# Rotation table: one more pause behind each quarter's stores; GLU products of the first tile one block later

## The chip, the core and the metric

The kernel runs on one core of a Trainium2 chip. The metric is device time in microseconds (us) from start to end of one execution. TensorE (PE) multiplies matrices and has a weight-load side (PEld), VectorE (DVE) and ScalarE (ACT) work on vectors, GpSimd (POOL) does little here, and SyncE (SP) issues nearly all DMAs, in order.

## The reference

A trunk of two layers, float32, 512 tokens of width 1024. Each layer is a SwiGLU feed-forward net (FFN, inner width 2752), a token mixer, and a second FFN; each of the three adds to the residual `x` behind an RMSNorm with shift, scale and gate from a conditioning vector. The second layer's mixer is a bidirectional complex-diagonal state-space model with a GLU:

```python
def s5_mixer(h, ...):
    u = h.reshape(Bsz, S, SSM_GROUPS, SSM_GROUP_DIM)          # 64 groups of 16
    y = d_skip * h
    for direction in range(N_DIRS):
        ar, ai, bb_re, bb_im = zoh_discretise(...)
        bu_re = jnp.einsum('bsgh,gph->bsgp', u, bb_re)        # and bu_im
        xr, xi = complex_linear_scan(ar, ai, bu_re, bu_im, reverse=(direction == 1))
        y = y + einsum(xr, c_re) - einsum(xi, c_im)
    y = jax.nn.gelu(y)
    z = y @ w_glu + b_glu                                     # 1024 x 2048
    return z[..., :D] * jax.nn.sigmoid(z[..., D:])
```

## The kernel before

Activations are held transposed, as 8 tiles of 128 channels by 512 tokens. A float32 product is made of three matmuls on operands that are split into a high and a low part (`mm3`, lines 684 to 686): high weight by low activation, high by high, low weight by high activation. For each weight tile the DMA brings `raw`, ACT casts the high part `whi` (line 677), and DVE makes the low part `wlo` by a subtraction (line 678). `raw` has 3 buffers, and `whi` and `wlo` have 4 each, so weights are prepared up to four tiles ahead of PE.

Every engine runs its instructions in the order in which the Python code emits them. Work for later stages is put between by generators: `prep()` advances the generator at the head of a list by one step (to its next `yield`), `mods()` makes one column of a modulation vector (line 635, with a DMA of `mw` behind it).

**The rotation table.** During the first FFN of layer 2, `rotation` builds the phases by which the mixer's states are turned. It works in four quarters. A quarter starts a tile `R` (one buffer, used by all four), doubles it six times with complex products (`cmul`, lines 127 to 129), and stores it into the DRAM scratch `rd` with four DMAs (line 279). Steps end at the `yield` inside the loops: the first step of a quarter holds the start and the doublings up to width 8 (24 small products behind two initial writes, L264 and L265 or L267 and L268); the three others hold six products of 256 columns each. Behind the last of these the generator is resumed once more: the stores go out, and the next quarter starts in the same step. The initial writes must wait until the stores have read `R`. Text below calls these steps *start step* and *product steps*.

In this FFN the hidden tiles are worked through in three parts (8, 7 and 6 tiles and a remainder of 64). In a part, first come the input products, 48 matmuls for each hidden tile, and then the output products, one for each of the 8 tiles of `x` (called d = 0 to 7), which in the second part have 21 matmuls each. In the output loop, each d has on DVE: the column of `mw`, the update of `x` (line 758), a step of the generator, and `wlo` of a later weight tile. The generator's later steps load the operators of the mixer's first blocks into SBUF (`rt`, `w1`, `w2`); `operators`, called behind d = 0 of the third part, runs what is left of it.

**The mixer.** `s5_mixer` goes over 8 blocks of 8 groups. `s5_state` of a block is 64 matmuls (line 1139), then on DVE the turning by `rt`, two scans (line 1161) and the turning back into `X`. `s5_out` (lines 1199 and 1207) makes the block's output from `u` and `X`; `s5_turn` (line 1222) transposes it, and ACT makes its GELU and the high part `hhi`; the low part `hlo` (line 1229) is put off to the end of the iteration (`self.lows`). Iteration b emits: output of block b, turning of block b-1, state of block b+2, the low part of block b-1, and then the share of block b-2 in the GLU's first tile: `glu_mm` with three matmuls for each of the two halves q. In iteration 7 the first five blocks' share of the GLU's second tile comes ahead of the output (30 matmuls). `glu` makes the rest.

Of the kernel before, what the change touches and what calls it, by code (L numbers as in the profile page):

```python
# [21 lines left out]
KD = D // P  # L22
# [42 lines left out]
class S5Prep:  # L65
# [155 lines left out]
    def rotation(self, pool):  # L221


        nc, I = self.nc, self.I
        v = nc.vector
        n = NG
        lam = pool.tile([P, 3, n], F32, name="lamB")
        nc.sync.dma_start(out=lam, in_=I["lamB"])
        yield
        S = lambda nm: pool.tile([P, n], F32, name=nm)  # L230
        dt, x1, th, si = (S(q) for q in ("dt", "x1", "th", "si"))
        self.vexp(pool, dt, lam[:, 2], n)
        yield
        v.tensor_tensor(out=x1, in0=lam[:, 0], in1=dt, op=ALU.mult)
        self.vexp(pool, self.rho, x1, n)
        for _ in range(3):
            v.tensor_tensor(out=self.rho, in0=self.rho, in1=self.rho, op=ALU.mult)
        v.tensor_tensor(out=th, in0=lam[:, 1], in1=dt, op=ALU.mult)
        v.tensor_scalar(out=th, in0=th, scalar1=8.0, scalar2=None, op0=ALU.mult)

        back = slice(n // 2, n)
        W = pool.tile([P, 2, 6, n], F32, name="W")
        self.vsincos(pool, W[:, 0, 0], si, th, n)
        yield
        v.tensor_copy(out=W[:, 1, 0, 0:n // 2], in_=si[:, 0:n // 2])
        v.tensor_scalar(out=W[:, 1, 0, back], in0=si[:, back], scalar1=-1.0, scalar2=None, op0=ALU.mult)
        yield
        for j in range(5):
            self.cmul(pool, W[:, 0, j + 1], W[:, 1, j + 1], W[:, 0, j], W[:, 1, j], W[:, 0, j], W[:, 1, j], [P, n])
        yield  # L250
        cur = W[:, 0, 0], W[:, 1, 0]
        for j in range(1, 6):
            o = [S(q) for q in (("dt", "x1"), ("th", "si"))[j % 2]]
            self.cmul(pool, *o, *cur, W[:, 0, j], W[:, 1, j], [P, n])
            cur = o
            if j % 2:
                yield
        nq = 4 * HB
        for q in range(NG // nq):
            gs = slice(q * nq, (q + 1) * nq)  # L260
            d, b0 = divmod(4 * q, NB)
            R = pool.tile([P, 2, nq, NC], F32, name="R")
            if d == 0:
                v.memset(R[:, 0, :, 0:1], 1.0)  # L264
                v.memset(R[:, 1, :, 0:1], 0.0)  # L265
            else:
                v.tensor_copy(out=R[:, 0, :, 0], in_=cur[0][:, gs])  # L267
                v.tensor_scalar(out=R[:, 1, :, 0], in0=cur[1][:, gs], scalar1=-1.0, scalar2=None, op0=ALU.mult)  # L268
            for j in range(6):
                w = 1 << j  # L270
                c = min(w, 16)
                bc = [W[:, r, j, gs].unsqueeze(2).to_broadcast([P, nq, c]) for r in range(2)]
                for i in range(0, w, c):
                    self.cmul(pool, R[:, 0, :, w + i:w + i + c], R[:, 1, :, w + i:w + i + c],
                              R[:, 0, :, i:i + c], R[:, 1, :, i:i + c], bc[0], bc[1], [P, nq, c])
                    if j > 2:
                        yield
            for b in range(4):
                nc.sync.dma_start(out=self.rd[b0 + b, :, d], in_=R[:, :, b * HB:(b + 1) * HB])

    def blocks(self, pool, psum, ident, eye16, dskip):

# [166 lines left out]
class Trunk:  # L449
# [865 lines left out]
    def s5_mixer(self, l, pool, pre, right, ops0, ut, rest):  # L1315
        nc, W = self.nc, self.W

        w1, w2, rt, w3, X = *ops0, {}
        pools = (pre, right)
        d0 = [pool.tile([P, 2, HB, NC + 1], F32, name=f"d{d}") for d in range(2)]  # L1320
        z = pool.tile([P, 2, HB, NC + 1], F32, name="z")
        wt = pool.tile([P, 2 * HB * (NC + 1) + 1], F32, name="ws")
        self.scan = d0, z, wt
        for t in (*d0, z):
            nc.gpsimd.memset(t[:, :, :, NC:NC + 1], 0.0)
        nc.gpsimd.memset(wt[:, 0:1], 0.0)
        for b in range(2, 4):
            w1[b] = self.s5_w1(pool, b, 2)
        r = self.s5_rstd(HALVES[1])
        for o in rest:  # L1330
            o()
        r()
        for b in range(len(ut), NB):
            ut[b] = self.s5_in(b)
        u = [self.s5_norm(ut[b], b) for b in range(2)]
        self.s5p = pools[0]
        self.gps = [[self.newps() for q in range(2)]]
        self.yv = []
        yj = {}
        for b in range(2):  # L1340
            X[b] = self.s5_state(pool, w1.pop(b), rt[b], u[b], b)
            w1[b + 4] = self.s5_w1(pools[b], b + 4)
            if b:
                while len(W.ready) < 4:
                    W.prep()
                yj[0] = self.s5_out(pool, w2.pop(0), w3.pop(0), ut[0], X.pop(0), 0)
            u.append(self.s5_norm(ut[b + 2], b + 2))
        self.lows = []
        self.gw = [[W.get(), W.get()] for m in range(2)]

        def turn(b):
            self.yv.append(tuple(t.rearrange("p (j c) -> p j c", j=L) for t in self.s5_turn(yj.pop(b))))

        for b in range(NB + 1):
            if 2 <= b <= 4:
                W.issue()
            if b == NB - 2:
                self.s5_spare(0)
            if b == NB - 1:
                self.s5_spare(1)  # L1360
                self.gps.append([self.newps() for q in range(2)])
                for q in range(2):
                    self.glu_mm(self.gps[1][q], self.gw[1][q], range(NB - 3))
            if 0 < b < NB:
                yj[b] = self.s5_out(pool, w2.pop(b), w3.pop(b), ut[b], X.pop(b), b)
            if b > 0:
                turn(b - 1)
            if b + 2 < NB:
                rt[b + 2] = self.s5_rt(pools[b % 2], b + 2)
                w3[b + 2] = self.s5_w3(pools[b % 2], b + 2)  # L1370
                w2[b + 2] = self.s5_w2(pools[b % 2], b + 2)
                if b + 4 < NB:
                    u.append(self.s5_norm(ut[b + 4], b + 4))
                X[b + 2] = self.s5_state(pool, w1.pop(b + 2), rt[b + 2], u[b + 2], b + 2)
                if b + 6 < NB:
                    w1[b + 6] = self.s5_w1(pool, b + 6, 2)
            while self.lows:
                self.lows.pop(0)()
            if b > 1:
                for q in range(2):  # L1380
                    self.glu_mm(self.gps[0][q], self.gw[0][q], [b - 2])

    def glu_mm(self, ps, w, ks, c0=0, c1=NC):
        n = L * (c1 - c0)
# [4 lines left out]
    def glu(self, l):  # L1389
# [4 lines left out]
        mm = self.glu_mm  # L1394

        def gate_in(m, ps):
            sg = self.tp.tile([P, T], F32, name="tmp")
            nc.scalar.activation(out=sg, in_=ps, func=AF.Sigmoid,
                                 bias=self.cols[:, C_GLUB + KD + m:C_GLUB + KD + m + 1], scale=1.0)
            return sg  # L1400
# [11 lines left out]
        def mods():  # L1412
            for _ in range(2):
                self.ahead = min(self.ahead, sum(not callable(t) for t in self.modq) - KD)
                if self.ahead or callable(self.modq[0]):
                    self.mods()

        for m in range(KD - 2):
            w = self.gw[m] if m < 2 else [W.get(), W.get()]
            ps = self.gps[m] if m < 2 else [self.newps() for q in range(2)]  # L1420
            if m == 0:
                for q in range(2):
                    mm(self.gps[1][q], self.gw[1][q], range(NB - 3, KD - 1))
                for q in range(2):
                    mm(ps[q], w[q], [KD - 1])
                sg = gate_in(m, ps[0])
                W.adv()
            else:
                ks = range(KD - 1 if m == 1 else 0, KD)
                mm(ps[0], w[0], ks)  # L1430
                sg = gate_in(m, ps[0])
                if m != 2:
                    W.adv()
                mods()
                mm(ps[1], w[1], ks)
            mix(m, ps[1], sg)
            if m != 2:
                W.adv()
            mods()

        a, b, hc = KD - 2, KD - 1, NC // 2
        w, sg = {}, {}
        for m in (a, b):
            w[m] = [W.get(), W.get()]
            ps = self.newps()
# [6 lines left out]
        for m in (a, b):  # L1452
            ps = self.newps()
            mm(ps, w[m][1], range(KD), 0, hc)
            mix(m, ps, sg[m], 0, hc)
        ps = {m: self.newps() for m in (a, b)}
# [310 lines left out]
```

## Time and profile before

| | us |
|---|---|
| median of three runs | 1734.79 |
| lowest and highest run | 1731.52 and 1735.48 |
| profiled execution | 1731.77 |
| its span, first to last instruction | 1729.8 |
| PE busy in the span | 1669.4 (97%) |
| DVE, ACT, POOL busy | 1186.2, 555.8, 100.1 |

PE is busy nearly always, so a wait of PE is what the end can be brought forward by; DVE has the second longest busy time, and in some stretches of the program more work than PE.

### The profile page before, as it was taken

To read this page: it belongs to the slowest core of one execution; us is meant where nothing else is said; L and a number is where in the kernel's file an instruction comes from. 1 tells how busy PE (TensorE), PEld (TensorE's weight loads), DVE (VectorE), ACT (ScalarE), POOL (GpSimd) and SP (SyncE) were. 2 spreads that over 40 slices of the span, in tenths; PEclk is the share of its full clock that TensorE was granted. 3 is DMA by queue.
4 is the path that set the end of the run, shared out by engine and by line. 5 is a ranking of instruction groups with operands and counts; after the bars stand their busy time and mean duration, and the time that the engine had idled before them with its cause. 6 is when DMAs were issued, how large, how long until landed. Compare 5 with 4: busy or idle time off the path is not lost.

```text
span 1729.8 us, 24992 instructions
## 1 busy us (share of the span) xinstructions
PE 1669.4 (97%) x9776; PEld 1393.1 (81%) x9776; DVE 1186.2 (69%) x2164; ACT 555.8 (32%) x845; POOL 100.1 (6%) x159
## 2 busy tenths in 40 slices
PE   8999999998999999999999997997899999999997
PEld 6888888888887887879888886886788988888886
DVE  7768777768989988877479667547956744334334
ACT  4321322255332222335322222354333532222222
POOL 0000000035011111120000000010000000000000
PEclk9999999999999999999999998998999999999998
DMA  9357557442599988872645455758643253233321
GB/s 379 128 161 262 176 175 254 147 130 84 167 277 303 283 263 257 257 230 88 231 134 170 155 162 172 255 175 269 228 171 98 88 168 98 97 92 93 113 74 56
DMA packets 129893, 307.92 MB, mean 178 GB/s; under 512 B 23488, under 2 KB 50496, under 8 KB 128752
## 3 DMA queue, kind: packets, MB, share of 16 engines
q1 hardware_dynamic: 126336, 299.45, 54.0%
q0 software_dynamic: 2896, 6.37, 1.2%
q8 instruction: 76, 1.25, 0.3%
q10 hardware_dynamic: 544, 0.52, 0.1%
q14 instruction: 41, 0.34, 0.1%
HBM read 278.63 MB, written 31.85 MB: 179 GB/s over the span
## 4 chain that ended last, share of the span: by engine, by line
PE 85%; DVE 9%; DMA 3%; ACT 1%; issue 1%; SPq 0%; DVEq 0%; ACTq 0%
PE ps L684 26%; PE ps L686 26%; PE ps L685 25%; PE ps L631 2%; DVE mw L635 1%; DMA mw<-modw 1%; DVE wlo L678 1%; PE ps L1207 1%; DVE tmp L739 1%; DMA rd<-R 1%; DVE ws L1161 1%; DVE hlo L742 1%; PE ps L341 1%; PE ps L1139 1%; PE ps L869 0%
## 5 line engine op out<-in xcount | busy, mean ns | idle before, releaser
L684 PE MATMUL ps<-hlo,whi 128*128 128x512 f32 (+3 forms) x1488 | 565.9, 380 | 11.0 <-DVE hlo L1229 7.5
L686 PE MATMUL ps<-hhi,wlo 128*128 128x512 f32 (+3 forms) x1488 | 562.3, 378 | 12.1 <-DVE wlo L678 12.0
L685 PE MATMUL ps<-hhi,whi 128*128 128x512 f32 (+3 forms) x1488 | 562.4, 378 | 0.0
L678 DVE TENSOR_TENSOR wlo<-raw,whi 128x1024 fp32r<-128x1024 f32 (+2 forms) x263 | 308.5, 1175 | 117.1 <-ACT whi L677 114.0
L677 ACT CAST whi<-raw 128x1024 fp32r<-128x1024 f32 (+2 forms) x273 | 273.2, 1010 | 344.3 <-PE ps L685 165.9
L684 PEld LDWEIGHTS ps<-hlo,whi 128*128 128x128 f32 x1488 | 280.9, 189 | 66.0 <-issue 10.6
L686 PEld LDWEIGHTS ps<-hhi,wlo 128*128 128x128 f32 x1488 | 281.0, 189 | 65.3 <-DVE wlo L678 13.8
L685 PEld LDWEIGHTS ps<-hhi,whi 128*128 128x128 f32 x1488 | 280.9, 189 | 51.2
L684 PE MATMUL ps<-glo,whi 128*128 128x512 f32 (+1 forms) x738 | 277.1, 375 | 1.1 <-DVE glo L678 1.1
L686 PE MATMUL ps<-ghi,wlo 128*128 128x512 f32 (+1 forms) x738 | 276.6, 375 | 0.0
L685 PE MATMUL ps<-ghi,whi 128*128 128x512 f32 (+1 forms) x738 | 276.6, 375 | 0.0
L677 ACT CAST ghi<-tmp 128x512 fp32r<-128x512 f32 x96 | 59.6, 620 | 465.8 <-DVE tmp L753 457.1
L635 DVE SCALAR_TENSOR_TENSOR mw<-mw,condb 128x1024 f32<-128x1024 f32 x144 | 174.8, 1219 | 21.6 <-DMA mw<-modw 21.4
L684 PEld LDWEIGHTS ps<-glo,whi 128*128 128x128 f32 x738 | 138.7, 188 | 29.4 <-DVE glo L678 1.5
L686 PEld LDWEIGHTS ps<-ghi,wlo 128*128 128x128 f32 x738 | 138.7, 188 | 27.5
L685 PEld LDWEIGHTS ps<-ghi,whi 128*128 128x128 f32 x738 | 138.7, 188 | 27.3
L753 DVE TENSOR_TENSOR tmp<-ps,tmp 128x512 f32<-128x512 f32 x88 | 60.5, 688 | 129.0 <-PE ps L686 117.0
L758 DVE SCALAR_TENSOR_TENSOR x<-ps,m,x 128x512 f32<-128x512 f32 (+1 forms) x107 | 74.1, 692 | 75.4 <-PE ps L686 75.2
L678 DVE TENSOR_TENSOR glo<-tmp,ghi 128x512 fp32r<-128x512 f32 x96 | 66.3, 692 | 60.6 <-ACT ghi L677 60.5
L702 ACT ACTIVATE tmp<-x 128x512 f32<-128x512 f32 (+3 forms) x69 | 34.8, 507 | 100.0 <-DVE x L758 60.0
L752 ACT ACTIVATE tmp<-ps 128x512 f32<-128x512 f32 x88 | 52.0, 591 | 5.7 <-PE ps L686 5.7
L704 DVE TENSOR_TENSOR acc<-acc,tmp 128x512 f32<-128x512 f32 (+1 forms) x43 | 29.7, 691 | 26.4 <-ACT tmp L702 25.7
(285 smaller groups left out, 1372.3 us busy)
## 6 DMA issues: line engine op xcount, KB each, us to landing
raw<-win SPq DMA_DIRECT2D x162, 512.0 KB, 3.8
mw<-modw SPq DMA_DIRECT2D x144, 512.0 KB, 4.9
raw<-wout SPq DMA_DIRECT2D x32, 512.0 KB, 3.6
raw<-wout SPq DMA_DIRECT2D x32, 448.0 KB, 3.4
raw<-wout SPq DMA_DIRECT2D x32, 384.0 KB, 3.2
ub<-ud SPq DMA_DIRECT2D x32, 256.0 KB, 5.7
ub<-s5bt SPq DMA_DIRECT2D x32, 256.0 KB, 5.8
w2d<-E SPq DMA_DIRECT2D x64, 128.0 KB, 5.2
```

What stands on the lines that cost most here:

```text
L631: nc.tensor.matmul(ps[m][q], lhsT=lhs[:, k], rhs=rhs, start=i == 3 * KD, stop=i == 1)
L635: self.nc.vector.scalar_tensor_tensor(out=w, in0=w, scalar=1.0, in1=self.condb, op0=ALU.mult, op1=ALU.mult, accum_out=dst)
L677: self.nc.scalar.copy(out=hi, in_=src)
L678: (eng or self.nc.vector).tensor_tensor(out=lo, in0=src, in1=hi.bitcast(F32), op=ALU.subtract)
L684: mm(ps, lhsT=hi[:, k], rhs=rhs[1][:, cs], start=start, stop=False)
L685: mm(ps, lhsT=hi[:, k], rhs=rhs[0][:, cs], start=False, stop=False)
L686: mm(ps, lhsT=lo[:, k], rhs=rhs[0][:, cs], start=False, stop=stop)
L702: nc.scalar.activation(out=sq[:, cs], in_=self.x[d][:, cs], func=AF.Square)
L704: (eng or nc.vector).tensor_tensor(out=self.acc[:, cs], in0=self.acc[:, cs], in1=sq[:, cs], op=ALU.add)
L752: nc.scalar.activation(out=t[0:n, cs], in_=pg[:, cs], func=AF.Silu)
L753: nc.vector.tensor_tensor(out=t[0:n, cs], in0=pu[:, cs], in1=t[0:n, cs], op=ALU.mult)
L758: self.nc.vector.scalar_tensor_tensor(out=self.x[d][:, cs], in0=ps[:, cs], scalar=scale[:, d:d + 1], in1=self.x[d][:, cs], op0=ALU.mult, o ...
```

## The change

Two edits, in three functions. In `rotation` a `yield` stands behind the four stores, so the start of the next quarter falls into the next step; each later step of this generator and of what follows it in the same list (four steps in all) moves back accordingly. In `s5_mixer`, iteration b now emits the share of block b-3 instead of b-2 (from b = 3 on), and `glu` emits that of the last two blocks instead of the last one. No instruction is added or taken away.

```diff
@@ rotation
             for b in range(4):
                 nc.sync.dma_start(out=self.rd[b0 + b, :, d], in_=R[:, :, b * HB:(b + 1) * HB])
+            yield
@@ s5_mixer
             while self.lows:
                 self.lows.pop(0)()
-            if b > 1:
+            if b > 2:
                 for q in range(2):
-                    self.glu_mm(self.gps[0][q], self.gw[0][q], [b - 2])
+                    self.glu_mm(self.gps[0][q], self.gw[0][q], [b - 3])
@@ glu
                 for q in range(2):
-                    mm(ps[q], w[q], [KD - 1])
+                    mm(ps[q], w[q], [KD - 2, KD - 1])
```

Lines behind 279 have numbers higher by one in the changed kernel.

On DVE, in the output products of the second part (`x_121`, `x_125`, `x_130` are tiles 0, 1 and 2 of `x`), before:

```order
L678 TENSOR_TENSOR wlo<-raw,whi 128x896
L635 SCALAR_TENSOR_TENSOR mw,m_579<-mw,condb 128x1024
L758 SCALAR_TENSOR_TENSOR x_121<-ps,m_575,x_121 128x512
L267 COPY R<-th 128x16
L268 TENSOR_SCALAR R<-si 128x16
L127 TENSOR_TENSOR ct<-R,W 128x16
```

The same place in the changed kernel, from the last products of the second quarter on:

```order
L127 TENSOR_TENSOR ct<-R,W 128x256
L128 TENSOR_TENSOR cu<-R,W 128x256
L129 TENSOR_TENSOR R<-ct,cu 128x16x16
L679 TENSOR_TENSOR wlo<-raw,whi 128x896
L636 SCALAR_TENSOR_TENSOR mw,m_579<-mw,condb 128x1024
L759 SCALAR_TENSOR_TENSOR x_125<-ps,m_575,x_125 128x512
L679 TENSOR_TENSOR wlo<-raw,whi 128x896
L636 SCALAR_TENSOR_TENSOR mw,m_579<-mw,condb 128x1024
L759 SCALAR_TENSOR_TENSOR x_130<-ps,m_575,x_130 128x512
L267 COPY R<-th 128x16
L268 TENSOR_SCALAR R<-si 128x16
```

The second quarter now ends at d = 0, its stores belong to d = 1, and the third quarter starts at d = 2 (before: d = 0). The third quarter's stores then fall to d = 6 and the fourth starts at d = 7 (before: d = 4).

On SP, the DMAs around the second quarter's stores, before:

```order
L419 DMA raw<-wout 128x896 x2
L487 DMA mw<-modw 128x1024
L279 DMA rd<-R 128x2x256 x4
L419 DMA raw<-wout 128x896
L487 DMA mw<-modw 128x1024
L419 DMA raw<-wint 128x1024
```

And from the same load of two weight tiles on in the changed kernel:

```order
L420 DMA raw<-wout 128x896 x2
L488 DMA mw<-modw 128x1024
L420 DMA raw<-wout 128x896
L488 DMA mw<-modw 128x1024
L279 DMA rd<-R 128x2x256 x4
L420 DMA raw<-wint 128x1024
```

The stores stand behind one more weight tile and one more `mw`, and right behind an `mw` as before. (The later loads of `rt`, `w1` and `w2` for the first blocks move from the third part's input products to its output products d = 0.)

On PE, in the mixer's iterations 2 and 3 (L1222 is the turning, L1139 the state, L1199 and L1207 the output), before:

```order
L1222 MATMUL ps<-ident,yj 64x64 x16
L1139 MATMUL ps<-hhi,w_10771 64x64 x32
L684 MATMUL ps<-hlo,whi 128x512
L685 MATMUL ps<-hhi,whi 128x512
L686 MATMUL ps<-hhi,wlo 128x512
L684 MATMUL ps<-hlo,whi 128x512
L685 MATMUL ps<-hhi,whi 128x512
L686 MATMUL ps<-hhi,wlo 128x512
L1199 MATMUL ps<-w_11112,hhi 64x128 x8
```

And in the changed kernel:

```order
L1223 MATMUL ps<-ident,yj 64x64 x16
L1140 MATMUL ps<-hhi,w_10771 64x64 x32
L1200 MATMUL ps<-w_11112,hhi 64x128 x8
L1208 MATMUL ps<-w_11114,X_11174 64x128 x16
L1208 MATMUL ps<-w_11114,X_11175 64x128 x16
L1208 MATMUL ps<-w_11114,X_11180 64x128 x16
L1208 MATMUL ps<-w_11114,X_11181 64x128 x16
L1223 MATMUL ps<-ident,yj 64x64 x16
L1140 MATMUL ps<-hhi,w_10842 64x64 x32
L685 MATMUL ps<-hlo,whi 128x512
```

Block 0's six matmuls, which stood ahead of the output of block 3, now stand behind the state of block 5; each later block's share moves by one iteration in the same way.

## Rows read from the trace of the kernel before

**Rows 1.** The page: busy us of each engine, share of the span, instructions.
```profile
PE 1669.4 (97%) x9776; PEld 1393.1 (81%) x9776; DVE 1186.2 (69%) x2164; ACT 555.8 (32%) x845; POOL 100.1 (6%) x159
```

**Rows 2.** DVE in time order: start, length, line, work [idle before it, and until what].
```profile
968.73 0.07 DVE L264 MEMSET R<- 128x16 f32 x1 [8.50 <-DMA rd<-R]
...
1012.13 0.08 DVE L635 DVE_READ_ACCUMULATOR mw<-mw,condb 128x1 f32 x1
1012.59 0.75 DVE L758 SCALAR_TENSOR_TENSOR x<-ps,m,x 128x512 f32<-128x512 f32 x1 [0.37 <-PE ps L686]
1020.07 0.18 DVE L267 COPY R<-th 128x16 f32<-128x16 f32 x1 [6.74 <-DMA rd<-R]
...
1025.36 1.08 DVE L678 TENSOR_TENSOR wlo<-raw,whi 128x896 fp32r<-128x896 f32 x1
...
1028.17 0.42 DVE L127 TENSOR_TENSOR ct<-R,W 128x256 f32<-128x256 f32 x1
...
1030.55 1.08 DVE L678 TENSOR_TENSOR wlo<-raw,whi 128x896 fp32r<-128x896 f32 x1
...
1043.09 0.74 DVE L758 SCALAR_TENSOR_TENSOR x<-ps,m,x 128x512 f32<-128x512 f32 x1
1051.52 0.18 DVE L267 COPY R<-th 128x16 f32<-128x16 f32 x1 [7.69 <-DMA rd<-R]
...
1056.79 1.22 DVE L678 TENSOR_TENSOR wlo<-raw,whi 128x1024 fp32r<-128x1024 f32 x1
```

**Rows 3.** PE in time order at two stretches of the first FFN of layer 2.
```profile
975.17 0.50 PE L686 MATMUL ps<-hhi,wlo 128*128 128x512 f32 x1 [0.70 <-DVE wlo L678]
...
1042.71 0.39 PE L685 MATMUL ps<-ghi,whi 128*128 128x512 f32 x1
...
1046.65 0.40 PE L684 MATMUL ps<-hlo,whi 128*128 128x512 f32 x1
1046.89 0.39 PE L685 MATMUL ps<-hhi,whi 128*128 128x512 f32 x1
1058.06 0.80 PE L686 MATMUL ps<-hhi,wlo 128*128 128x512 f32 x1 [10.78 <-DVE wlo L678]
...
1062.37 0.40 PE L684 MATMUL ps<-hlo,whi 128*128 128x512 f32 x1
```

**Rows 4.** SP in time order: the second quarter's stores (start, time of issuing).
```profile
1012.62 2.87 SPq L279 DMA_DIRECT2D rd<-R  x4
```

**Rows 5.** PE in time order in the mixer.
```profile
1210.94 1.98 PE L1207 MATMUL ps<-w,X 64*64 64x128 f32 x64 [2.84 <-DVE X L1148]
...
1224.66 0.77 PE L684 MATMUL ps<-hlo,whi 128*128 128x512 f32 x1 [6.06 <-DVE hlo L1229]
...
1227.49 1.98 PE L1199 MATMUL ps<-w,hhi 128*64 128x128 f32 x16
...
1237.69 1.09 PE L1199 MATMUL ps<-w,hhi 128*64 128x128 f32 x16
...
1264.94 0.50 PE L684 MATMUL ps<-hlo,whi 128*128 128x512 f32 x1 [1.48 <-DVE hlo L1229]
```

**Rows 6.** Stretches: length, PE, PEld, DVE, ACT, POOL busy, granted TensorE clock, DMA.
```profile
1210.00:1215.00 5.00, 3.29 (x112) 3.05 (x116) 4.86 (x10) 1.85 (x4) 0.00 (x0) 1.00 0.85 311
...
1220.00:1225.00 5.00, 0.34 (x1) 0.37 (x2) 4.86 (x9) 0.00 (x0) 0.00 (x0) 0.76 0.70 265
```

**Rows 7.** DVE in time order in the mixer.
```profile
1223.83 0.68 DVE L1229 TENSOR_TENSOR hlo<-tmp,hhi 128x512 fp32r<-128x512 f32 x1
...
1245.38 1.89 DVE L1148 TENSOR_TENSOR tmp<-ps,rt 128x512 f32<-128x512 f32 x3 [0.37 <-PE ps L1139]
...
1253.12 1.03 DVE L1148 TENSOR_TENSOR X<-ws,rt 128x512 f32<-128x512 f32 x2
...
1264.20 0.69 DVE L1229 TENSOR_TENSOR hlo<-tmp,hhi 128x512 fp32r<-128x512 f32 x1
```

**Rows 8.** The page, DMA issues: KB each, median us from issue to landing.
```profile
w<-w1d SPq DMA_DIRECT2D x8, 1024.0 KB, 7.9
```

## The prediction

> **What bounds the kernel now.** I read the page first: PE is busy in 97% of the span [rows 1], so an edit pays only where it removes a pause of PE or a stretch in which PE runs at the lower clock. Then I looked for the work that is moved in the list of waits and in the order of time of DVE and PE.
>
> In the first FFN of layer 2 DVE stands still three times for the stores of `R`: 8.50, 6.74 and 7.69 us [rows 2]. What PE makes of it is very uneven [rows 3]. The first stall lies in the input products, where a hidden tile gives DVE 11 us, and leaves 0.70 us on PE. The second costs PE nothing by itself. The third lies in the same output loop, and by then the weights that were prepared ahead are used up: PE stops at 1047.3 for 10.78 us, waiting for a `wlo`. Behind the pause PE needs 4.31 us for ten matmuls (1058.06 to 1062.37); eighteen of the same shape before it take 4.18 us (1042.71 to 1046.89), 0.232 each. So ten cost 2.0 us too much: that is the lower of the two clock levels, granted after the long pause.
>
> In the mixer PE waits twice for an `hlo` that DVE makes late, 6.06 and 1.48 us [rows 5]. DVE has no such pauses there: 4.86 of 5 us busy at the stretches shown [rows 6]. It takes 10.1 us per block (four blocks from the first `hlo` at 1223.83 to the fifth at 1264.20 [rows 7]) and PE's share of a block is less, so up to the last state DVE sets the pace. The first pause also takes PE to the lower level: the mean grant is 0.76 in 1220 to 1225 [rows 6], the six GLU matmuls behind it take 2.83 us instead of 1.39, and the sixteen of L1199 1.98 instead of 1.09 [rows 5]: 2.3 us in all.
>
> **Edit 1, the pause behind the stores.** It adds no work; four generator steps hold only DMA issues. What counts is how much of the `R` wait fits behind other work.
>
> Price of the wait: from the end of the `mw` column behind which the stores are issued to the release of `R` it takes 7.9 us for the second quarter (1012.2 to 1020.07) and 8.4 for the third (1043.1 to 1051.52) [rows 2]; the four issues themselves take 2.87 [rows 4]. I use 8.2.
>
> First to second quarter: a whole hidden tile, 48 matmuls or 11.1 us, now lies between. The wait goes, and with it PE's 0.70.
>
> For the output loop I replay DVE on the old times. Its pieces [rows 2]: `wlo`, `mw` and `x` together 2.81 (1025.36 to 1028.17), a product step 2.38 (1028.17 to 1030.55), a start step 5.27 (1051.52 to 1056.79). PE ends output d = 0 at 1012.6 and starts the third part at 1046.65 [rows 3], so a d takes 4.87. Before, DVE had 2.81 + 2.38 = 5.19 in most d, more than PE's 4.87, and over 12 us in the two with a start step and a stall.
>
> - d = 0: `x` ends at 1013.3, product step 1015.7, `mw` 1017.8. The second quarter's stores go out there and release `R` at 1026.0.
> - d = 1: no product step. d = 2: `x` waits for PE, 1023.0; the start step waits from there to 1026.0, a stall of 3.0 where 6.74 stood, and ends at 1031.3.
> - d = 3 to 5: product steps end at 1036.5, 1041.6 and 1046.9. The `wlo` for the third part's first tile, for which PE stood 10.78 us, is made behind d = 4's step: 1042.8, and PE wants it at 1046.65. No pause.
> - Behind d = 5 come two casts' low parts, 2.4 us: 1049.4, wanted at 1052.2. The third quarter's stores go out there and release `R` at 1057.6.
> - d = 7: `x` at 1053.1, stall of 4.5, start step to 1062.9, its `wlo` 1064.0. PE wants that one after three input products of 24 matmuls, at 1046.65 + 3 x 5.57 = 1063.4. PE waits 0.6 us. From there a hidden tile gives DVE 11.1 us for, by my estimate from these pieces, some 9 (two `wlo`, a column of `mw`, a product step and two operations of half a tile), so it gains ground.
>
> With 7.9 the last wait is 0.3, with 9.0 it is 1.4; at under 7.5 there is none. Sum of edit 1: 10.8 + 2.0 + 0.7 - 0.6 = 12.9 us, bounds 11.5 and 13.6.
>
> The generator's end moves too. `rt`, `w1` and `w2` for the first blocks (2.5 MB) are now issued with d = 0 of the third part. One such transfer of 1 MB lands after 7.9 us [rows 8], the three take at most some 20 one behind another. That loop starts near 1131 of the old times (1058.06 + 5.6 for the remainder + six tiles of 11.1); the mixer's output of block 2 stands at 1210.94 [rows 5], so that of block 1 near 1200, and it wants them some 60 us after the issue. Behind them on SP stand weight tiles of this output loop; up to three raw and four split tiles of 20 matmuls (4.6 us) lie ahead of PE, 32 us of cover. Cost nothing; without the cover it would be the 20.
>
> **Edit 2, GLU products one block later.** PE's work is the same. In iteration 2 PE no longer waits for the first `hlo` (DVE makes it at 1223.83, behind state 3 [rows 7]) but goes on from 1218.6 with the output of block 3, as far as `X` is there. The waits 6.06 and the slow 2.3 go at that place, but PE cannot keep all of it, since DVE sets the pace of `X` and `hlo`. The new place to look at is iteration 7: the 30 matmuls for the GLU's second tile include block 4, whose `hlo` ends at 1264.9 [rows 7]. Before, PE came there with block 4's six products of the first tile and all 30 still to do (36). After, the first tile's products for block 3 and the first twelve of the 30 lie ahead of the wait, and behind it come the other 18 and, later in the program, block 4's six. So from this instant to the end of the first tile PE has 54 products instead of 66 left to do. 12 x 0.232 = 2.8 us. DVE arrives 0.4 us sooner, since its wait of 0.37 for PE at state 6 [rows 7] goes. Sum 3.2 us.
>
> Does PE get there in time? The output of block 6 needs the second direction's `X`, made from 1253.1 less 0.4 [rows 7]. Its second half is 1.98 [rows 5], the turning about 1 (an estimate, like L1199's sixteen, 1.09 [rows 5]), then 6 + 12 products, 4.2: about 1260.6. So PE pauses some 3.8 us before the `hlo` at 1264.5: the wait of 1.48 becomes longer, and the gain is what was done before it. Bounds: 0, if the transfers for `X` or `w2` came late as DMA is at 0.70 to 0.85 of its time there [rows 6]; 4.0, if the slow ramp at 1264.94 is also missed. I take 3.2.
>
> That pause of 3.8 us lies between one of 2.84, in whose stretch the grant stays at 1.00, and one of 6.06, in which it falls [rows 5, 6]. If it falls, it costs up to what it cost at 1224.66, 2.3 us, and edit 2 leaves 0.9. I take no fall, as the nearer row.
> The Trainium skill, page "TensorE: Matmul & The Clock Gate", section "HAM oscillation — how this bites in real kernels", warns that a PE left idle between bursts returns to half clock and pays for it at each burst; by that rule this pause would be hit and the sum would be 13.8 instead of 16.1. The pauses of 6.06 and 10.78 agree with it, that of 2.84 does not show it; no run yet shows one of 3.8.
>
> **Sum.** 12.9 + 3.2 = 16.1 us. The profiled execution, 1731.77, would become 1715.7. It lies 3.0 under the median of the runs shown, 1734.79, from which the same step gives **1718.7 us**.
>
> **Rivals.**
> 1. *The store wait bites again.* The pause gives 4.87 us of cover in the output loop and the wait is 8.2; stalls of 3.0 and 4.5 remain, and my margin in front of 1064.0 is used up. If the stores land 4 us later, behind the weight tile and the `mw` in front of them, PE waits 4.6 there and gets the lower clock once more (2.0): edit 1 gives 13.5 - 6.6 = 6.9, both 10.1: 1724.7. For it: no margin. Against: the order on SP right ahead of the stores is as before, and the two measured prices lie 0.5 apart.
> 2. *The lower clock in the mixer*, as above: 1721.0.
> 3. *The GLU edit gives nothing*, because DVE's pace moves the wait whole: 1721.9. Against it: 12 products less are left behind the same `hlo`.
> 4. *No change*: the start of a quarter waits as long as before since the stores also move. It would need DVE to be that much late before d = 0, which its wait for PE at 1012.59 [rows 2] contradicts. 1734.8.
> 5. *Slower*: the 2.5 MB in the third part's output loop hold up its weight tiles. It decides once they take over 32 us; to turn 16.1 us into a loss of 3.5 they would have to take 52 instead of 20: 1738.3 or more.
>
> **How the numbers follow.** Forecast, both edits pay (11 to 18 us): 0.67. Rival 1: 0.11. Rival 2: 0.10. Rival 3: 0.05. Rival 4: 0.04. Rival 5: 0.03. A measurement of this kernel tells about 0.2%, 3.5 us, from no change. Faster by more: 0.93, within: 0.04, slower: 0.03. The range takes in the forecast with its bounds (edit 1 11.5 to 13.6, edit 2 0 to 4.0: 1717.2 to 1723.3), the rivals 2 and 3, and the runs' own scatter of 3 us below the median: 1714 to 1724. Outside lie most of rival 1, and rivals 4 and 5.
>
> **What would show it.** Right: no wait of PE for a `wlo` near 1047, granted clock 1.00 there; DVE waits at L267 of some 3 and 4.5 us and none at L264; PE without a wait at the first `hlo`, one wait of 3 to 4 us for the fifth block's `hlo` within the 30 products; DVE's spacing of the scans as before. Wrong: a wait of PE over 2 us in the third part's input products, a pause at that `hlo` with the clock falling, or a PE wait for weights in the third part's output loop. The least sure step is the replay of d = 7, then PE's arrival in iteration 7.

## The result and the profile after

The changed kernel takes **1719.21 us** (median of four runs, 1717.77 to 1720.51), the kernel before, run beside it, 1735.13 (1731.52 to 1735.48): a ratio of 0.9913, 95% interval 0.9895 to 0.993. The forecast was 1718.7 in a range of 1714 to 1724. The profiled execution took 1717.77, its span 1715.7, 14.1 less than before.

The page of the changed kernel, busy us of each engine:

```profile
PE 1670.2 (97%) x9776; PEld 1395.9 (81%) x9776; DVE 1187.0 (69%) x2164; ACT 556.2 (32%) x845; POOL 100.0 (6%) x159
```

Beside [rows 1] no engine has less work: what went are pauses of PE. To see where, I lay three updates of `x` of the two traces beside each other, which both kernels make with the same instructions: one in the rotation's first quarter, ahead of its stores, the last one ahead of the mixer, the first one behind it. DVE in time order, before:

```profile
938.56 0.74 DVE L758 SCALAR_TENSOR_TENSOR x<-ps,m,x 128x512 f32<-128x512 f32 x1
...
1173.72 0.48 DVE L758 SCALAR_TENSOR_TENSOR x<-ps,m,x 128x256 f32<-128x256 f32 x1
...
1452.02 0.75 DVE L758 SCALAR_TENSOR_TENSOR x<-ps,m,x 128x512 f32<-128x512 f32 x1 [1.68 <-PE ps L686]
```

And in the changed kernel, with what answers to [rows 2] between them:

```profile
940.25 0.75 DVE L759 SCALAR_TENSOR_TENSOR x<-ps,m,x 128x512 f32<-128x512 f32 x1
...
970.51 0.07 DVE L264 MEMSET R<- 128x16 f32 x1 [0.89 <-DMA rd<-R]
...
1026.55 0.18 DVE L267 COPY R<-th 128x16 f32<-128x16 f32 x1 [2.73 <-DMA rd<-R]
...
1042.22 1.22 DVE L679 TENSOR_TENSOR wlo<-raw,whi 128x1024 fp32r<-128x1024 f32 x1
...
1058.13 0.19 DVE L267 COPY R<-th 128x16 f32<-128x16 f32 x1 [4.31 <-DMA rd<-R]
...
1162.16 0.48 DVE L759 SCALAR_TENSOR_TENSOR x<-ps,m,x 128x256 f32<-128x256 f32 x1
...
1437.86 0.75 DVE L759 SCALAR_TENSOR_TENSOR x<-ps,m,x 128x512 f32<-128x512 f32 x1 [1.68 <-PE ps L687]
```

The three stand at +1.7, -11.6 and -14.2 against before. So this execution lost 1.7 us ahead of the change (single executions differ there, as said below), won **13.2** in the FFN with the rotation and **2.6** in the mixer, and nothing behind it. 13.2 + 2.6 = 15.8 stands beside the forecast sum of 16.1; what the 2.6 are made of comes with edit 2 below. The stalls of 8.50, 6.74 and 7.69 have become 0.89, 2.73 and 4.31, and the `wlo` for which PE stood 10.78 us is made at 1042.22, before PE asks for it. The granted clock, the third figure from the end as in [rows 6], shows the other part of the gain; before, and behind it the changed kernel:

```profile
1055.00:1060.00 5.00, 1.94 (x5) 1.57 (x6) 4.86 (x12) 0.00 (x0) 0.00 (x0) 0.50 0.16 31
```

```profile
1055.00:1060.00 5.00, 5.00 (x24) 4.14 (x23) 1.67 (x12) 0.00 (x0) 0.00 (x0) 1.00 0.99 340
```

PE of the changed kernel in time order, first the only wait between 940 and 1100, then the mixer:

```profile
1064.70 0.50 PE L687 MATMUL ps<-hhi,wlo 128*128 128x512 f32 x1 [0.38 <-DVE wlo L679]
...
1198.60 5.21 PE L1208 MATMUL ps<-w,X 64*64 64x128 f32 x128 [2.84 <-DVE X L1149]
...
1251.92 0.50 PE L685 MATMUL ps<-hlo,whi 128*128 128x512 f32 x1 [3.68 <-DVE hlo L1230]
1252.26 0.40 PE L686 MATMUL ps<-hhi,whi 128*128 128x512 f32 x1
1252.50 0.40 PE L687 MATMUL ps<-hhi,wlo 128*128 128x512 f32 x1
...
1253.02 0.63 PE L686 MATMUL ps<-hhi,whi 128*128 128x512 f32 x1
1253.44 0.63 PE L687 MATMUL ps<-hhi,wlo 128*128 128x512 f32 x1
...
1256.00 0.54 PE L687 MATMUL ps<-hhi,wlo 128*128 128x512 f32 x1
1256.39 0.40 PE L685 MATMUL ps<-hlo,whi 128*128 128x512 f32 x1
...
1257.87 1.09 PE L1200 MATMUL ps<-w,hhi 128*64 128x128 f32 x16
```

The waits of 6.06 and 1.48 for `hlo` [rows 5] are gone; one of 3.68, for block 4, stands in iteration 7. The matmuls behind it start 0.24 apart at first, then 0.39 to 0.43 from 1253.02 to 1256.39, and about 0.24 again from there, so that eighteen take 5.95 (1251.92 to 1257.87) instead of 18 x 0.232 = 4.18. The stretches show why:

```profile
1195.00:1200.00 5.00, 2.16 (x41) 1.92 (x41) 4.02 (x8) 4.43 (x9) 0.00 (x0) 0.83 0.90 309
...
1245.00:1250.00 5.00, 3.24 (x15) 2.34 (x13) 4.83 (x9) 1.69 (x3) 0.00 (x0) 1.00 0.00 0
1250.00:1255.00 5.00, 3.08 (x9) 2.46 (x10) 4.74 (x7) 0.00 (x0) 0.00 (x0) 0.79 0.16 33
1255.00:1260.00 5.00, 5.00 (x66) 3.95 (x69) 0.00 (x0) 0.00 (x0) 0.00 (x0) 0.87 0.52 180
```

Part of 1250 to 1260 runs at the lower of the two levels. It costs 5.95 - 4.18 = 1.8 us.

The low parts of blocks 0 and 4 divide the mixer's stage. DVE of the changed kernel:

```profile
1211.50 0.68 DVE L1230 TENSOR_TENSOR hlo<-tmp,hhi 128x512 fp32r<-128x512 f32 x1
...
1251.18 0.68 DVE L1230 TENSOR_TENSOR hlo<-tmp,hhi 128x512 fp32r<-128x512 f32 x1
```

Against [rows 7], 0.8 of the 2.6 us are won ahead of block 0's `hlo`, 0.7 between the two and 1.1 behind block 4's. Up to block 0's `hlo` both kernels emit the mixer in the same order, so edit 2 accounts for 1.8 of the 2.6.

### The profile page after: what moved, and what is told of

Its sections match the earlier page's. It is cut to its first block, busy times and chain, and to the rows that moved or that the text cites. A ratio compares the mean times of both kernels' runs of the same rounds, so it can differ in the third digit from the quotient of the medians.

```text
span 1715.7 us, 24999 instructions
## 1 busy us (share of the span) xinstructions
PE 1670.2 (97%) x9776; PEld 1395.9 (81%) x9776; DVE 1187.0 (69%) x2164; ACT 556.2 (32%) x845; POOL 100.0 (6%) x159
## 4 chain that ended last, share of the span: by engine, by line
PE 80%; DVE 10%; DMA 5%; issue 2%; ACT 1%; SPq 1%; DVEq 0%; ACTq 0%
PE ps L685 25%; PE ps L687 25%; PE ps L686 24%; PE ps L632 2%; DMA mw<-modw 2%; DVE wlo L679 1%; DVE ws L1162 1%; DVE mw L636 1%; DVE tmp L740 1%; DMA rd<-R 1%; DMA sraw<-win 1%; DVE X L1149 1%; DVE hlo L743 1%; DVE tmp L1149 1%; DVE z L1149 1%
```

## The experiments

Every kernel was timed against the kernel before. For each, the stages are taken from the same three updates of `x` in its profiled execution, in us against the trace of before:

| | ahead | FFN | mixer | of it from block 0's `hlo` on |
|---|---|---|---|---|
| changed kernel | +1.7 | -13.2 | -2.6 | -1.8 |
| the same again (e9) | +1.3 | -12.6 | -2.2 | -1.9 |
| edit 1 alone (e1) | +2.4 | -13.1 | 0.0 | -0.1 |
| edit 2 alone (e2, again) | +2.6 | +1.1 | -3.1 | -1.9 |
| pause ahead of the stores (e3) | +2.8 | -4.4 | -3.3 | -3.2 |
| block 4 late (e4) | +4.3 | -12.4 | -6.3 | -5.7 |
| two blocks late (e5) | +4.1 | -11.8 | +0.9 | +0.9 |
| two pauses (e6) | +0.9 | -14.0 | -1.8 | -0.5 |
| e4 and e6 together (e7) | +6.3 | -14.0 | -7.2 | -7.1 |
| e4, `hlo` on GpSimd (e8) | +3.9 | -12.3 | -5.2 | |

The column "ahead" has nothing to do with any edit; its spread of 5 us is why one profiled execution's total says little here and its stages say more. All ten are positive: the execution of before that was profiled, 1731.77 in all, was the quickest of the eleven there. The mixer's part ahead of block 0's `hlo`, which no edit touches either, scatters by 1.4 us (from -1.3 to +0.1), so edits in the mixer are compared by the last column. It has no value for e8, where another engine makes this `hlo`.

**Edit 1 alone.** Of the change only:

```diff
+            yield        # rotation, behind the four stores
```

> Edit 1 alone. My theory (each edit pays by itself, in its own stretch): 13.0 us less than the kernel before, about 1722 us; the trace shows stalls of some 2.7 and 4.3 us at the third and fourth quarter's start as in the changed kernel, no wait of PE near 1047, and in the mixer the old waits of 6.1 and 1.5 us for the low parts of blocks 0 and 4. Rival (the two edits share one gain, since both shorten waits of PE for a late DVE): the time is that of the changed kernel within 2 us, about 1719.

Measured: 1719.95, beside 1733.43 before; ratio 0.9918 (0.9905 to 0.9932). The median lies near the number of either theory; the stages tell them apart: the FFN alone gives 13.1, the mixer nothing, and there PE's old pauses stand. The list of PE's waits of this kernel, 1190 to 1270 (total us, times, longest):

```profile
PE ps L685 <- DVE hlo L1230: 7.0, 2, 5.4
```

**Edit 2 alone**, twice, since the first run left no profile that could be compared:

```diff
-            if b > 1:
+            if b > 2:
...
-                    self.glu_mm(self.gps[0][q], self.gw[0][q], [b - 2])
+                    self.glu_mm(self.gps[0][q], self.gw[0][q], [b - 3])
...
-                    mm(ps[q], w[q], [KD - 1])
+                    mm(ps[q], w[q], [KD - 2, KD - 1])
```

> Edit 2 alone. My theory: 2.5 to 3 us less than before, about 1732 us; the waits of PE for R's stores stay (10.8 us near 1047), the wait for block 0's low part is gone, and PE waits 3.7 us for block 4's low part inside the thirty products, with the granted clock falling behind it (0.79 in five us). Rival (edit 2 gives nothing, DVE's pace moves the wait whole): 1735 us, and the first matmul behind the thirty products stands no earlier against DVE's last scan than before.

> Edit 2 alone once more, for its trace (that of glu_only was disturbed). My theory: in the stage of the mixer 2.2 to 3.3 us less than in the kernel before, nothing in the FFN ahead of it; wait of 10.8 us for a weight near 1047 as before, wait of 3.7 us for block 4's low part. Rival (edit 2 gives nothing): the mixer's stage takes as long as before within 0.5 us.

Measured: 1732.23, ratio 0.9989 (0.998 to 0.9998), and 1732.42, ratio 0.9985 (0.9975 to 0.9994). The mixer gives 3.1 us, 1.9 of them from block 0's `hlo` on, and the FFN none; that it took 1.1 longer, with the instructions of before, is scatter. PE's row in the mixer of the second run:

```profile
1266.71 0.50 PE L684 MATMUL ps<-hlo,whi 128*128 128x512 f32 x1 [3.30 <-DVE hlo L1229]
```

The edits add: FFN 13.1 in e1 and 1.9 in e2's mixer from block 0's `hlo` on make 15.0, both together 15.0 and, in e9, 14.5. In whole times edit 2 is small: 1.9 and 2.6 us alone, and on top of edit 1 it does not stand out (0.9918 in e1, 0.9913 and 0.9908 with both, inside each other's intervals).

**The pause ahead of the stores.** DVE's work moves exactly as in the change, only the stores stay with the next start:

```diff
+            yield
             for b in range(4):
                 nc.sync.dma_start(out=self.rd[b0 + b, :, d], in_=R[:, :, b * HB:(b + 1) * HB])
-            yield
```

> The changed kernel, but with the pause of the generator ahead of the four stores instead of behind them: DVE's instructions stand in the same order as in the changed kernel, only the stores go out one step later on SP, in the step in which the next quarter starts. My theory (what pays is that the stores' 8 us run behind another step's work): stalls of 7 to 8.5 us come back at all three starts; by the replay PE then waits some 6 us for the weight behind the fourth quarter's start and runs about 2 us at the lower clock, so about 8 us more than the changed kernel, 1727 us. Rival (what pays is that the start steps moved to other places of the output loop, so that DVE's load is better spread): the same as the changed kernel within 1.5 us, about 1719.

Measured: 1726.69, ratio 0.9958 (0.9945 to 0.997). DVE in time order, and behind it PE, of this kernel:

```profile
979.35 0.07 DVE L264 MEMSET R<- 128x16 f32 x1 [8.58 <-DMA rd<-R]
...
1031.09 0.18 DVE L267 COPY R<-th 128x16 f32<-128x16 f32 x1 [6.13 <-DMA rd<-R]
...
1066.55 0.18 DVE L267 COPY R<-th 128x16 f32<-128x16 f32 x1 [8.21 <-DMA rd<-R]
```

```profile
1073.08 0.79 PE L687 MATMUL ps<-hhi,wlo 128*128 128x512 f32 x1 [7.17 <-DVE wlo L679]
```

All three stalls are back at the size of [rows 2], and PE waits 7.17 us. Where the start steps stand is worth 4.4 of the FFN's gain; the other 8 to 9 come from the work that lies between the stores and the next start.

**Block 4's share of the second tile behind the wait**, in the changed kernel:

```diff
-                    self.glu_mm(self.gps[1][q], self.gw[1][q], range(NB - 3))
+                    self.glu_mm(self.gps[1][q], self.gw[1][q], range(NB - 4))
...
-                    mm(self.gps[1][q], self.gw[1][q], range(NB - 3, KD - 1))
+                    mm(self.gps[1][q], self.gw[1][q], range(NB - 4, KD - 1))
```

> The changed kernel, and of the thirty products for the GLU's second tile ahead of block 7's output only those of blocks 0 to 3 (24); block 4's six move to the place behind the last block, where the later blocks' already stand. My theory (PE's pause of 3.7 us there and the 1.8 us at the lower clock behind it are lost time, and nothing else is late behind it): no wait for block 4's low part, granted clock 1.00, and 4 to 5.5 us less than the changed kernel, about 1714 us. Rival (the pause only moves on, to X of block 7 or the low parts of blocks 6 and 7, as DVE sets the pace): within 1.5 us of the changed kernel, with a new wait of PE of 2 us or more before the first tile of the GLU ends.

Measured: 1715.6, ratio 0.9888 (0.9873 to 0.9903). No wait for an `hlo` is left, and the clock stays up. The stretch of this kernel in which the changed one paused:

```profile
1250.00:1255.00 5.00, 5.00 (x23) 4.10 (x23) 4.83 (x11) 1.84 (x3) 0.00 (x0) 1.00 0.00 0
```

The mixer gives 6.3, some 4 more than in the changed kernel. That is less than the pause of 3.68 and the 1.8 behind it. In this execution PE stands once ahead of the place, for no cause that the profile names:

```profile
1240.96 0.92 PE L1140 MATMUL ps<-hhi,w 128*64 128x64 f32 x23 [1.32 <-issue]
```

In e7, whose mixer has the same instructions, that stand is missing and the last column gives 7.1, 5.3 more than in the changed kernel: the pause and the slow stretch were both still to be had.

**One block later still**, in the changed kernel:

```diff
-            if b > 2:
+            if b > 3:
...
-                    self.glu_mm(self.gps[0][q], self.gw[0][q], [b - 3])
+                    self.glu_mm(self.gps[0][q], self.gw[0][q], [b - 4])
...
-                    mm(ps[q], w[q], [KD - 2, KD - 1])
+                    mm(ps[q], w[q], [KD - 3, KD - 2, KD - 1])
```

> The changed kernel with the first GLU tile's share moved by one more block: iteration b emits block b-4's six products, and the last three blocks' share comes behind the last block. My theory (what counts is how many products still lie behind block 4's low part, as DVE sets when that comes: 66 before, 54 in the changed kernel, 60 here): PE reaches the wait 1.4 us sooner, waits some 5 us instead of 3.7, and the first tile ends 1.4 us later than in the changed kernel, with up to 1 us more if the granted clock stays low for longer; so 1720.5 us where the changed kernel has 1719. Rival (each block by which the products move takes a wait away, so later is better): 1 to 2 us less than the changed kernel.

Measured: 1722.32, ratio 0.9929 (0.9917 to 0.9942), 3.5 above the changed kernel in the same set of runs (e9, 1718.8). PE's waits for `X` from 1180 to 1300, of e5 and behind it of e9, and then PE of e5 at block 4's `hlo`:

```profile
PE ps L1208 <- DVE X L1149: 13.0, 12, 2.7
```

```profile
PE ps L1208 <- DVE X L1149: 9.9, 10, 2.8
```

```profile
1256.61 0.79 PE L685 MATMUL ps<-hlo,whi 128*128 128x512 f32 x1 [3.68 <-DVE hlo L1230]
...
1263.81 1.09 PE L1200 MATMUL ps<-w,hhi 128*64 128x128 f32 x16
```

The pause for `hlo` did not grow, against what I expected. PE had less to do between the outputs and stood 3.1 us more for `X` instead, and the six products that were taken from there (6 x 0.232 = 1.4) came behind the last state, where nothing hides them. The lower clock held on longer, too: the eighteen products behind the pause take 7.20 us, in the changed kernel 5.95. 1.4 and 1.3 make the 2.7 by which the last column differs. That the longer fall comes from this edit is not shown; e6, which has not got it, has 6.90 there.

**A second pause**, in the changed kernel:

```diff
             yield
+            yield
```

> The changed kernel with two pauses behind the stores instead of one. My theory (what one pause leaves is the DVE stalls of 7 to 8 us at the last two starts, of which PE feels 0.4 to 1.9): the FFN's stage takes 0.4 to 1.5 us less than in the changed kernel, whole time about 1718 us, no stall for the stores. Rival (the last quarter's stores now go out just ahead of the first rt load, and SP waits there for them): a wait of PE for weights in the third part's output loop, and 1 us or more slower.

Measured: 1717.33, ratio 0.99 (0.9886 to 0.9915). The lists of waits have no stall of DVE for `R` and no wait of PE for a `wlo` in this FFN; the stage gives 14.0 here and in e7, against 11.8 to 13.2 in the six executions with one pause. What was left behind the one pause was thus worth 0.8 to 2.2 us of the end. In whole times that does not stand out (0.99 against 0.9913 and 0.9908).

**Both mends together.** The edits of e4 and e6.

> The kernel with block 4's six products moved behind the last block (fifth_late), and two pauses behind the stores of a quarter instead of one. My theory (one pause covers 4.9 of the 8.2 us in the output loop, and what is left costs PE only the 0.4 to 1.2 us seen behind the fourth quarter's start): no stall of DVE for the stores, no wait of PE for a split weight in the third part, and 0 to 1.5 us less than fifth_late, about 1715 us. Rival (the stalls left on DVE cost more than PE's records show, or the later stores, behind which SP must wait before it loads the first rt, hold up the weights of the output loop): 2 us or more less, or 2 us or more slower.

Measured: **1712.17** (1711.18 to 1717.25), ratio 0.9874 (0.9861 to 0.9888): 6.6 under the changed kernel in the same set of runs. It is the lowest time here, though its interval overlaps that of e4. The stages add again, FFN as in e6 and the mixer 0.9 beyond e4.

**The low parts of blocks 0 to 4 on GpSimd**, in e4:

```diff
-        self.lows.append(lambda: nc.vector.tensor_tensor(...))
+        eng = nc.gpsimd if len(self.yv) < 5 else nc.vector
+        self.lows.append(lambda: eng.tensor_tensor(...))
```

> The kernel fifth_late, with the low parts of the mixer's blocks 0 to 4 made by GpSimd instead of VectorE. My theory (VectorE sets the pace of the mixer up to the last state): the blocks come 0.6 us closer together, 9.6 instead of 10.2 where a low part lay between them, and the mixer ends 1.5 to 3 us sooner than in fifth_late. Rival (PE or the loads set the pace, or GpSimd's work on the same memory slows VectorE by as much): the distance of the scans stays within 0.2 us, and the time within 1 us.

Measured: 1717.18, ratio 0.9898 (0.9885 to 0.9912): no gain over e4, rather a loss of 1 in the mixer (5.2 against 6.3). The moved operation holds up DVE. The same two operations in e8, beside GpSimd, and in e9, without it:

```profile
1210.93 1.29 POOL L1231 TENSOR_TENSOR hlo<-tmp,hhi 128x512 fp32r<-128x512 f32 x1 [6.66 <-ACT hhi L1229]
1211.02 2.09 DVE L1149 TENSOR_TENSOR X<-ws,rt 128x512 f32<-128x512 f32 x2
```

```profile
1208.16 1.02 DVE L1149 TENSOR_TENSOR X<-ws,rt 128x512 f32<-128x512 f32 x2
```

2.09 instead of 1.02: what DVE was spared, some 0.6 us a block, it more than lost by waiting. The Trainium skill, page "SBUF — State Buffer", section "SBUF: two separate sides", says that DVE operations with two SBUF inputs and GpSimd operations that read SBUF take turns at one pair of ports, each for its whole length; the rows agree. The scans of blocks 4 and 5, on DVE, in e8 and behind it in e9:

```profile
1219.76 1.23 DVE L1162 TENSOR_TENSOR_SCAN ws<-d,z 128x519 f32<-128x519 f32 x1
...
1230.46 1.23 DVE L1162 TENSOR_TENSOR_SCAN ws<-d,z 128x519 f32<-128x519 f32 x1
```

```profile
1216.44 1.23 DVE L1162 TENSOR_TENSOR_SCAN ws<-d,z 128x519 f32<-128x519 f32 x1
...
1226.66 1.23 DVE L1162 TENSOR_TENSOR_SCAN ws<-d,z 128x519 f32<-128x519 f32 x1
```

They stand 10.70 apart instead of 10.22: neither closer, as my theory had it, nor unchanged, as the rival had it. Whether the mixer would end sooner with less work on DVE, this run has not tested.

**The changed kernel again**, as the measure for e5, e7 and e8.

> The changed kernel itself, beside the other three on the same chip: 0.991 of the kernel before, as in its first measurement; every other run of this call is held against it.

Measured: 1718.8, ratio 0.9908 (0.9895 to 0.9922), before 1734.66. The pause for block 4's `hlo` is 3.66 here.

## Why the prediction was right, point by point

**Edit 1 was right, and for the reason given.** Forecast 12.9; the FFN gave 13.2, 12.6 and, with the edit alone, 13.1. The replay said stalls of none, 3.0 and 4.5 and a wait of 0.6 for the `wlo` behind the last; measured were 0.89, 2.73, 4.31 and 0.38. The price of the `R` wait held: in the output loop it takes 7.6 us both times from the first of the four stores to the release. SP of the changed kernel:

```profile
962.34 2.74 SPq L279 DMA_DIRECT2D rd<-R  x4
...
1018.95 2.97 SPq L279 DMA_DIRECT2D rd<-R  x4
...
1050.54 2.66 SPq L279 DMA_DIRECT2D rd<-R  x4
```

1018.95 to 1026.55 and 1050.54 to 1058.13, where [rows 4] and [rows 2] have 1012.62 to 1020.07, which is 7.45. That the first stall is 0.89 and not none is a small miss that cost PE nothing: I counted PE's 11.1 us of a hidden tile as cover, but DVE came to the start step 7.3 us after the first store, and the release took 8.2 (962.34 to 970.51).

The least sure step, the replay of d = 7, was as narrow as I said. Over the six executions with one pause PE's wait for that `wlo` was 0.38, 0.99 (e9), 0.50 (e1), 1.24 (e4), 1.87 (e5) and 1.32 us (e8). The longest, of e5:

```profile
1068.64 0.50 PE L687 MATMUL ps<-hhi,wlo 128*128 128x512 f32 x1 [1.87 <-DVE wlo L679]
```

Wait and gain of the FFN add up to 13.6 us, within 0.1, in each of the six; the forecast had 10.8 + 2.0 + 0.7 = 13.5 less the wait. So the sum of edit 1's terms holds, and only the size of the last wait moves from execution to execution. Rival 1 (the wait bites again, 4.6 us and a fall of the clock) falls with these waits, behind which the grant stayed at 1.00, rival 4 with e1. e3 shows which part of the edit pays: 4.4 us come from the later start steps, the other 8 to 9 from the work that lies under the stores.

**The transfers for the mixer are hidden**, as costed. Rival 5 needed a wait of PE for weights in the third part's output loop; the 2.5 MB are issued there (SP of the changed kernel), and from 1100 to 1170 the list of PE's waits names no weight tile.

```profile
1122.62 0.95 SPq L1126 DMA_DIRECT2D rt<-rd  x1
1123.62 0.43 SPq L1095 DMA_DIRECT2D w<-w1d  x1
...
1128.45 0.43 SPq L1101 DMA_DIRECT2D w<-w2d  x1
```

**Edit 2: the mechanism was right, one step in it wrong.** Forecast 3.2; from block 0's `hlo` on the edit gave 1.8, 1.9 and, alone, 1.9. PE's first pause goes, and the one in iteration 7 was forecast at 3.8 and is 3.68. The step that failed is "I take no fall, as the nearer row": the clock did fall behind that pause, which the prediction itself lists among the signs of being wrong. e3, whose mixer has the same instructions, shows the forecast as it was meant. DVE, PE and the clock of e3:

```profile
1261.80 0.68 DVE L1230 TENSOR_TENSOR hlo<-tmp,hhi 128x512 fp32r<-128x512 f32 x1
...
1447.12 0.75 DVE L759 SCALAR_TENSOR_TENSOR x<-ps,m,x 128x512 f32<-128x512 f32 x1 [1.69 <-PE ps L687]
```

```profile
1262.53 0.50 PE L685 MATMUL ps<-hlo,whi 128*128 128x512 f32 x1 [3.46 <-DVE hlo L1230]
...
1266.84 1.09 PE L1200 MATMUL ps<-w,hhi 128*64 128x128 f32 x16
```

```profile
1260.00:1265.00 5.00, 2.47 (x11) 2.05 (x12) 4.96 (x8) 0.00 (x0) 0.00 (x0) 1.00 0.15 20
```

The grant stayed at 1.00, the eighteen products took 4.31 us instead of 5.95, and behind block 4's `hlo` 2.5 us were won, where the forecast had 2.8; with the fall it was 1.1 or 1.2. In all four, block 4's `hlo` came 0.7 us sooner after block 0's instead of 0.4 (39.7 us, before 40.4 [rows 7]). So the mechanism gave 3.2 us without the fall, and the fall took 1.3 of them, where rival 2 had put up to 2.3; in e6, where the eighteen took 6.90, it took 2.7.

That the sum stayed close is in part luck. By their stages the two edits gave 15.0 and 14.5 us, the medians differ by 15.9, and the forecast was 16.1. In the profiled execution the mixer's 2.6 came closer to 3.2 by the 0.8 that were won ahead of block 0's `hlo`, where edit 2 changes nothing.

The nearer row, the pause of 2.84 [rows 5], could not carry the step. Over the eleven profiled executions the pause before the first `X` output of block 2, of 2.75 to 2.84 us (2.22 in e7), kept a grant of 1.00 in three (the kernel before, e5, e9) and lost it in eight, the changed kernel's own first execution among these (the 2.84 at 1198.60, grant 0.83) and e9, the same program, not. The pause before block 4's `hlo`, 3.30 to 3.68 us in six executions, lost it in five; in e3 it was 3.46 and the grant stayed 1.00. So one execution's row said what could happen, not what would. The rule of the Trainium skill in the prediction (page "TensorE: Matmul & The Clock Gate", section "HAM oscillation — how this bites in real kernels") thus agreed in most executions, not in all; the sum of 13.8 that stood beside it was too low, since in the changed kernel the fall cost 1.3 us of the end and not 2.3. Rival 3 (edit 2 gives nothing) falls with e2.

## What to carry to other kernels

Where an engine runs in order, a wait for a store's end delays everything queued behind it: put the store early and the reuse of its buffer late, with other work of that engine between, and count how much of the wait that work covers. Product work that stands in a stretch paced by another engine costs nothing and should stay there (e5), but not in front of something that the other engine has yet to deliver (e4). A profile of one execution shows one draw of the granted clock: cost a pause both with and without the fall.

## What the runs showed of the hardware

The grant falls after the pause, not only in it: behind the pause that ended at 1251.92, with the grant at 1.00 through 1245 to 1250, the first matmuls still follow each other at full speed, and the slow ones begin about 1 us after PE resumed. Equal pauses at the same place of the same program end in both ways (2.84 at a grant of 0.83 in the changed kernel, 2.83 at 1.00 in e9); what decides is open. The fall at that earlier place cost nothing that the stages show (mixer -2.6 with it, -2.2 without): PE's waits for `X` from 1180 to 1300 sum to 6.7 us with it and 9.9 without, so the slow work filled time in which PE would have stood. Why single executions differ by 0.9 to 6.3 us ahead of the change was not tried.
